# Seventy-two gathered tokens instead of eighty in a PEER expert layer, and a weight buffer moved to a later stage

## The chip, the cores and the metric

The kernel runs on one core of one Trainium2 chip. The metric is the device time of one execution in microseconds; the median of three runs of the kernel before is 1536.64 us (1535.43 to 1538.62). Five engines work at once, each through its own queue in program order: PE multiplies matrices, DVE and ACT work on elements, POOL does elementwise work and issues gathers, and SP only issues DMAs.

## The reference, cut to what matters

One layer of a decoder trunk on 512 tokens of width 1024: an input projection, 16 Mamba-2 heads and 8 latent attention heads, an output projection, a LayerNorm, and then the PEER channel mixer, which is where the change lies:

```python
def block(xb):                       # 128 tokens
    q = (xb @ w_query).reshape(T, PEER_HEADS, 2, PEER_HALF_DIM)
    s = jnp.einsum('thkd,hknd->thkn', q, sub_keys)
    sv, si = lax.top_k(s, K)
    ...
    expert_idx = jnp.take_along_axis(cand_i, top_pos, axis=-1)
    gate = jax.nn.softmax(top_s, axis=-1)
    u = jnp.take(u_table, expert_idx, axis=0)
    act = jax.nn.gelu(jnp.einsum('td,thkd->thk', xb, u), approximate=False)
    v = jnp.take(v_table, expert_idx, axis=0)
    return jnp.einsum('thk,thkd->td', gate * act, v)
```

Each token picks 8 x 16 = 128 of 16384 experts; each expert has a row of 1024 numbers in u_table and one in v_table. LayerNorm of 2^0.25 times the input plus this gives the output.

## The kernel before

The mixer is computed in two ways. The last 128 tokens are done by gathering: for each of their 128 choices a row of U per token is fetched (`row<-u,ix`, line 1587), multiplied and summed on DVE, and later a row of V likewise. The first 384 tokens (NT) are done densely, as if every token used all experts: 128 chunks of 128 experts, each chunk first "U" (the product of the chunk's 1024 x 128 weights with the tokens, GELU behind it) and later "V" (gate times GELU, times the chunk's V rows, summed over all chunks in six PSUM banks). The gates lie in a matrix of 384 tokens by 16384 experts that the kernel builds between the two from one-hot products.

Of the 384 dense tokens, the last UG = 80 have no U product. Their 128 choices each are handled by gathered U rows: UA = 64 tokens and UB = 16 tokens are spread over the partitions so that 64 + 16 = 80 gathers of 128 rows (`urow`, line 1150) and as many DVE dot products (line 1159) do all 80 x 128 of them; the results are folded into the gates. So a U product is NX = 384 - 80 = 304 columns wide. `NU` = 320 columns of each chunk's activations are kept, and the columns from NX to NU are filled with ones (line 1451).

**Products.** Every matrix product is done in fp32 quality by three passes (`mm3`, lines 90 to 92): each operand is split into a high part (ACT, line 131, `wih`) and a low part (subtraction, line 145 on DVE or POOL, line 143 on POOL, `wil`). A U chunk is 8 x 3 = 24 matmuls of 304 columns, a V chunk 18 of 512.

**The weight stream.** `Stream` loads the 512 KB weight tiles through SP's queue (`wir`, line 113). A load is issued when the subtraction of an earlier tile has freed its buffer: `self.loads(n + 1 + self.rawb)`. There are three rotating raw buffers. A fourth, `wirx` in pool `wsr`, exists from the query projection on, and then `rawb` is 4: every fourth tile uses it.

**The stages.** After the mixer's head come: the query projection with the top-16 search on DVE (about 405 to 530 us); a decode of the search's result (to about 605 us); the building of the gate matrix in 48 steps (`build_g`, to about 830 us); and the V stage to the end. U chunks fill PE beside the search, the decode and the building: 88 of them (PRE) are done before the V stage. The other 40 are done in it, one before each V chunk from V chunk GAP on, where GAP = 88 - LEAD - 1.

**Where the activations stay.** LEAD = KEEP + MORE + REST chunks of U results are held on the chip in three pools that open one after another; KEEP = 47 of them in the first. What has no place is written to DRAM (`asp<-aout`, line 1456) and read back later (line 1434): 41 chunks.

**A step of `build_g`.** DVE makes one-hot matrices (`oj`, line 1264, and `g`, line 1270) for the next step; in some steps (LOWA) ACT makes a part of `g` (line 1274). PE does 16 small f16 matmuls (lines 1308 and 1309), ACT moves their sums to `stg`, and ACT's queue stores them (`gsp<-stg`). A number of gathered dots follows on DVE: `for _ in range(3 - n % 2)`. How many U half chunks stand in a step is set by `drive`, which compares two running sums of estimated time and takes at least `least[0]` half chunks. While `beside[0]` is set (n < 32), the low part of a U tile that falls due is left to POOL: DVE writes one element of the tile (memset, line 142) so that POOL starts (line 143) while DVE is at the dots that follow. In the steps after the last dot `ug_head` puts the dots' results, which go through DRAM (`hbd`, `uw`), into the gates; its transpose is line 1197.

Before the dots, the x rows of the 16 UB tokens are spread over the partitions by DMAs into unused columns of XT: `for i in range(0, 128, UB)` (line 1542), eight DMAs on SP's queue.

Of the kernel before, what the change touches and what calls it, by code (L numbers as in the profile page):

```python
# [29 lines left out]
SCALE = 192.0 ** -0.5  # L30
NT = 384
UA = 64
UB = 16
UG = UA + UB
NX = NT - UG
NU = 320
ND = NU // 32
PIECES = 3
FIRST = 44
KEEP = 47  # L40
MORE = 12
REST = 8
LEAD = KEEP + MORE + REST
PRE = 88
# [9 lines left out]
ENDU = 9  # L54
WV = 0.86
BESIDE = 32
BSTEP = 25
GST = (1, 3, 5, 7)
LOWA = (*range(2, 32, 2), 34)
SCB = 6  # L60
# [11 lines left out]
def tile_block(ctx: ExitStack, tc: tile.TileContext, I, out):  # L72
# [6 lines left out]
    def pool(name, bufs=1, **kw):  # L79
        p = tc.alloc_tile_pool(name=name, bufs=bufs, **kw)  # L80
        opened.append(p)
        return p
# [162 lines left out]
    acd = dram.tile([64, 128], F32, name="acd")  # L245
    ixd = dram.tile([UB, 128], I32, name="ixd")
    hbd = dram.tile([128, UB], F32, name="hbd")
    asp = dram.tile([PRE - KEEP, 128, NU], F32, name="asp")

# [25 lines left out]
    beside = [False]  # L275
# [14 lines left out]
    win = Stream(wst, "wi", items, [128, 1024], raw=3, la=2, lo=lambda n: lo_on[0])  # L290
# [841 lines left out]
    def ug_index(tmp):  # L1132
# [5 lines left out]
        V.tensor_copy(UR["ix"][UA:], ix[UA:, UA:])  # L1138
        G.dma_start(ixd, ix[UA - UB:UA])
        G.dma_start(UR["g"][:UA], f(ijg[UA:, 2]))  # L1140
        G.dma_start(UR["g"][UA:], f(ijg[UA - UB:UA, 2]))
        for n in range(UROWS):
# [10 lines left out]
    def ug_dots():  # L1153
# [3 lines left out]
        for n in range(UG):  # L1157
# [4 lines left out]
            if n == 1:  # L1162
                G.dma_start(UR["ixb"], bass.AP(tensor=ixd.tensor, offset=ixd.offset, ap=[[UB, 128 // UB], [128, UB], [1, UB]]))
            if n == UA + 3:
# [76 lines left out]
    def build_g():  # L1241
# [44 lines left out]
        for n in range(48):  # L1286
            if n == BSTEP:
                next(dots)
# [40 lines left out]
            if late and late[0][0] <= n:  # L1329
                _, k, z = late.pop(0)  # L1330
# [10 lines left out]
                    lump += 1.1  # L1341
            lump += (1.45 if n + 1 in LOWA else 1.95) if n < 47 else 0.1
            if n < 32:
                keep, least[0], beside[0] = least[0], 1 + len(UO) if n % 2 == 0 else 0, n < BESIDE
                yield lump
                least[0], lump, beside[0] = keep, 0.0, False
            for _ in range(3 - n % 2):
                lump += next(dots, 0.0)
            for _ in range({34: 2, 35: 2, 36: 1}.get(n, 0)):
                lump += next(head)  # L1350
            yield lump

# [40 lines left out]
    close(mix)  # L1393
    close(zx)
    win.xp = pool("wsx")
    win.xr = pool("wsr")
    win.ha = 1
    aps = [pool("act")]
    ALL = [aps[0].tile([128, FIRST, NU], F32, name="acts")]
# [3 lines left out]

    sizes = (KEEP, MORE, REST)
    away = []
# [22 lines left out]
    def refill():  # L1428
        while away:
# [3 lines left out]
            c = away.pop(0)  # L1433
            G.dma_start(t, asp[c - KEEP])
            ACT[c] = t

    UO = {}

    def u_half(c, e, psum=None):
# [5 lines left out]
        if e:  # L1445
# [6 lines left out]
            else:  # L1452
                t = out_.tile([128, NU], F32, name="aout", bufs=3)
                A.activation(t[:, :NX], ps, AF.Gelu)  # L1454
                A.activation(t[:, NX:], one, AF.Copy)
                nc.sync.dma_start(asp[c - KEEP], t)
                away.append(c)
# [34 lines left out]
    least = [0]  # L1492
# [72 lines left out]
    B1 = gb.tile([128, 32, 8, 2], F16, name="unit")  # L1565
    least[0] = 1
    drive(build_g())
    close(gs[1], ga, gs0_, gb)
    GS = [-1, 0, 0]
# [52 lines left out]

    vst = pool("vst")
    aps.append(pool("act3"))
    fill = gather()
    next(fill)
    gt = {}
# [301 lines left out]
```

## Time and profile before

| | us |
|---|---|
| median of 3 runs | 1536.64 |
| the profiled execution, its own time | 1537.87 |
| span of its trace (first to last instruction) | 1536.1 |
| PE busy | 1503.6 |
| DVE busy | 1349.1 |
| ACT busy | 768.7 |
| POOL busy | 706.1 |

The span is what the trace shows; 1.77 us of the execution lie around it. PE's matmuls are pipelined, so one that the trace shows as 300 ns long may be followed by the next after 138 ns, and short waits can hide in PE's busy time. The granted TensorE clock has a mean of 0.996 over the span.

### The profile page before, as it was taken

To read this page: it belongs to the slowest core of one execution; us is meant where nothing else is said; L and a number is where in the kernel's file an instruction comes from. 1 tells how busy PE (TensorE), PEld (TensorE's weight loads), DVE (VectorE), ACT (ScalarE), POOL (GpSimd) and SP (SyncE) were. 2 spreads that over 40 slices of the span, in tenths; PEclk is the share of its full clock that TensorE was granted. 3 is DMA by queue.
4 is the path that set the end of the run, shared out by engine and by line. 5 is a ranking of instruction groups with operands and counts; after the bars stand their busy time and mean duration, and the time that the engine had idled before them with its cause. 6 is when DMAs were issued, how large, how long until landed. Compare 5 with 4: busy or idle time off the path is not lost.

```text
span 1536.1 us, 24889 instructions
## 1 busy us (share of the span) xinstructions
PE 1503.6 (98%) x8664; PEld 1316.1 (86%) x8664; DVE 1349.1 (88%) x2672; ACT 768.7 (50%) x1541; POOL 706.1 (46%) x522
## 2 busy tenths in 40 slices
PE   9999999999999999988999999999999999999997
PEld 7787888888888999988988988999998888888886
DVE  8979768746799999988999688999999999999998
ACT  5564477742433455665766644444444434443342
POOL 0000032420244523767852365667666676776630
PEclk9999999999999999999999999999999999999999
DMA  6243122475423676999998999999999999999994
GB/s 261 96 145 104 57 71 60 111 251 161 155 76 90 141 259 234 361 350 407 410 390 281 343 399 376 399 398 399 394 399 399 398 396 385 388 383 361 390 326 151
DMA packets 159118, 428.27 MB, mean 279 GB/s; under 512 B 18056, under 2 KB 59984, under 8 KB 158736
## 3 DMA queue, kind: packets, MB, share of 16 engines
q1 hardware_dynamic: 98336, 211.72, 39.4%
q0 software_dynamic: 55104, 196.65, 33.6%
q10 hardware_dynamic: 5552, 18.31, 3.1%
q8 instruction: 68, 1.11, 0.3%
q14 instruction: 58, 0.48, 0.1%
HBM read 393.37 MB, written 31.08 MB: 276 GB/s over the span
## 4 chain that ended last, share of the span: by engine, by line
PE 72%; DVE 11%; DMA 10%; issue 4%; ACT 3%; POOL 1%; ACTq 0%; DVEq 0%; POOLq 0%; SPq 0%
PE va L1724 9%; PE va L1720 9%; PE va L1721 9%; PE pu L91 6%; PE pu L90 6%; PE pu L92 6%; DMA row<-v,ix 3%; PE pw L90 3%; PE pw L92 3%; PE pa L91 3%; PE pw L91 3%; PE pa L92 3%; PE pa L90 3%; DVE wil L145 2%; DMA row<-u,ix 2%
## 5 line engine op out<-in xcount | busy, mean ns | idle before, releaser
L131 ACT ACTIVATE wih<-wir 128x1024 fp32r<-128x1024 f32 (+2 forms) x269 | 276.9, 1031 | 115.6 <-PE va L1724 40.7
L92 PE MATMUL pu<-XT,wil 128*128 128x304 f32 x1000 | 300.3, 300 | 4.0 <-POOL wil L143 2.6
L145 DVE TENSOR_TENSOR wil<-wir,wih 128x1024 fp32r<-128x1024 f32 (+1 forms) x212 | 256.0, 1209 | 54.2 <-ACT wih L131 34.4
L1721 PE MATMUL va<-wil,Ph 128*128 128x512 f32 x726 | 283.0, 390 | 1.6 <-DVE wil L145 1.5
L1587 POOL DMA_INDIRECT row<-v,ix x128 | 218.3, 1706 | 101.4 <-DVE ac L1608 81.4
L90 PE MATMUL pu<-XT,wih 128*128 128x304 f32 x824 | 250.0, 303 | 2.0 <-ACT aout L1454 1.6
L91 PE MATMUL pu<-XT,wih 128*128 128x304 f32 x824 | 249.6, 303 | 0.0
L1587 POOL DMA_INDIRECT row<-u,ix x128 | 175.1, 1368 | 138.3 <-DVE row L1602 71.5
L92 PEld LDWEIGHTS pu<-XT,wil 128*128 128x128 f32 x1000 | 188.3, 188 | 4.8 <-POOL wil L143 2.9
L1720 PE MATMUL va<-wih,Ph 128*128 128x512 f32 x486 | 189.1, 389 | 0.0
L1608 DVE SCALAR_TENSOR_TENSOR ac<-row,hd,ac 128x1024 f32<-128x1024 f32 x128 | 164.3, 1284 | 4.0 <-DMA row<-v,ix 2.3
L1602 DVE SCALAR_TENSOR_TENSOR row<-row,XT 128x1024 f32<-128x1024 f32 x128 | 154.1, 1223 | 11.6 <-DMA row<-u,ix 11.5
L1721 PEld LDWEIGHTS va<-wil,Ph 128*128 128x128 f32 x726 | 136.3, 188 | 30.2 <-DVE wil L145 3.3
L90 PEld LDWEIGHTS pu<-XT,wih 128*128 128x128 f32 x824 | 155.4, 189 | 4.7 <-ACT aout L1454 1.9
L91 PEld LDWEIGHTS pu<-XT,wih 128*128 128x128 f32 x824 | 155.8, 189 | 1.6
L1724 PE MATMUL va<-wih,Pl 128*128 128x512 f32 x486 | 149.9, 390 | 0.4 <-DVE Pl L1711 0.2
L145 POOL TENSOR_TENSOR wil<-wir,wih 128x1024 fp32r<-128x1024 f32 (+3 forms) x37 | 77.8, 2111 | 144.5 <-ACT wih L131 125.8
L1703 ACT ACTIVATE Ph<-P 128x384 fp32r<-128x384 f32 x121 | 63.0, 520 | 149.6 <-DVE P L1680 139.4
L1159 DVE SCALAR_TENSOR_TENSOR urow<-urow,xp 128x1024 f32<-128x1024 f32 x80 | 95.2, 1218 | 15.7 <-DMA urow<-u,uix 12.2
L1724 PEld LDWEIGHTS va<-wih,Pl 128*128 128x128 f32 x486 | 91.1, 188 | 19.9 <-DVE Pl L1711 1.2
L1720 PEld LDWEIGHTS va<-wih,Ph 128*128 128x128 f32 x486 | 91.2, 188 | 18.1
L1150 POOL DMA_INDIRECT urow<-u,uix x64 | 78.6, 1228 | 40.2 <-DVE urow L1159 23.1
(527 smaller groups left out, 3449.5 us busy)
## 6 DMA issues: line engine op xcount, KB each, us to landing
wir<-ut SPq DMA_DIRECT2D x106, 512.0 KB
wir<-v SPq DMA_DIRECT2D x86, 512.0 KB
wirx<-v SPq DMA_DIRECT2D x42, 512.0 KB
gt<-gsp SPq DMA_DIRECT2D x63, 256.0 KB
wir<-wo SPq DMA_DIRECT2D x26, 512.0 KB
wirx<-ut SPq DMA_DIRECT2D x22, 512.0 KB
gsp<-stg ACTq DMA_DIRECT2D x24, 448.0 KB
wir<-wf SPq DMA_DIRECT2D x18, 512.0 KB
```

Source lines behind the costliest of these rows:

```text
L90: T.matmul(ps, lh, rh, start=start, stop=False)
L91: T.matmul(ps, lh, rl, start=False, stop=False)
L92: T.matmul(ps, ll, rh, start=False, stop=stop)
L131: A.activation(h, r, AF.Copy)
L145: self.lo(n).tensor_tensor(l, r, h, op=OP.subtract)
L1159: V.scalar_tensor_tensor(r, r, 1.0, UR["xp"], op0=OP.mult, op1=OP.mult, accum_out=hd[:, n:n + 1] if n < UA else hb[:, n - UA:n - UA + 1])
L1587: G.indirect_dma_start(out=R[s], out_offset=None, in_=I["u"] if s < 128 else I["v"], in_offset=bass.IndirectOffsetOnAxis(ap=ix3[:, s % 128 ...
L1602: V.scalar_tensor_tensor(wide(r), wide(r), 1.0, x3, op0=OP.mult, op1=OP.mult, accum_out=hd[:, s:s + 1])
L1608: V.scalar_tensor_tensor(ac, r, hd[:, s - 128:s - 127], ac, op0=OP.mult, op1=OP.add)
L1720: T.matmul(va[b][e], Ph[b], h[:, cs], start=c == 0, stop=False)
L1721: T.matmul(va[b][e], Ph[b], l[:, cs], start=False, stop=False)
L1724: T.matmul(va[b][e], Pl[b], h[:, cs], start=False, stop=c == 127)
```

## The change

- UB is 8 instead of 16: 72 tokens of the 384 have gathered U rows, in 64 + 8 = 72 gathers and dots. The U products are 312 wide, and 8 columns are filled with ones. The x rows of the 8 tokens need 16 DMAs on SP's queue instead of 8, each half as large.
- KEEP is 50 instead of 47: 38 chunks go through DRAM instead of 41, and GAP is 17 instead of 20.
- The pool `wsr` is opened at the V stage, not after the mixer's output projection: in the query, decode and building stages there are three raw buffers, in the V stage four.
- In `build_g` a step has 2 dots, and 3 where n is a multiple of four. The number of U half chunks that stand ahead of the dots comes from the running sums alone; the POOL subtractions follow from it. BSTEP (where an extra dot is taken) is 28 instead of 25, and the last two parts of `ug_head`, its transpose and what follows it, come one step later (n = 36 and 37).

```diff
@@ -30,14 +30,14 @@
 SCALE = 192.0 ** -0.5
 NT = 384
 UA = 64
-UB = 16
+UB = 8
 UG = UA + UB
 NX = NT - UG
 NU = 320
 ND = NU // 32
 PIECES = 3
 FIRST = 44
-KEEP = 47
+KEEP = 50
 MORE = 12
 REST = 8
 LEAD = KEEP + MORE + REST
@@ -54,7 +54,7 @@
 ENDU = 9
 WV = 0.86
 BESIDE = 32
-BSTEP = 25
+BSTEP = 28
 GST = (1, 3, 5, 7)
 LOWA = (*range(2, 32, 2), 34)
 SCB = 6
@@ -1341,12 +1341,12 @@
                     lump += 1.1
             lump += (1.45 if n + 1 in LOWA else 1.95) if n < 47 else 0.1
             if n < 32:
-                keep, least[0], beside[0] = least[0], 1 + len(UO) if n % 2 == 0 else 0, n < BESIDE
+                keep, least[0], beside[0] = least[0], 0, n < BESIDE
                 yield lump
                 least[0], lump, beside[0] = keep, 0.0, False
-            for _ in range(3 - n % 2):
+            for _ in range(2 + (n % 4 == 0)):
                 lump += next(dots, 0.0)
-            for _ in range({34: 2, 35: 2, 36: 1}.get(n, 0)):
+            for _ in range({34: 2, 35: 1, 36: 1, 37: 1}.get(n, 0)):
                 lump += next(head)
             yield lump
 
@@ -1393,7 +1393,6 @@
     close(mix)
     close(zx)
     win.xp = pool("wsx")
-    win.xr = pool("wsr")
     win.ha = 1
     aps = [pool("act")]
     ALL = [aps[0].tile([128, FIRST, NU], F32, name="acts")]
@@ -1622,6 +1621,7 @@
 
     vst = pool("vst")
     aps.append(pool("act3"))
+    win.xr = pool("wsr")
     fill = gather()
     next(fill)
     gt = {}
```

On DVE, at the fourth and fifth steps of `build_g`, the order before (L1159 is a dot, L142 the memset that lets POOL start a low part, L145 a low part on DVE):

```order
L1264 TENSOR_TENSOR oj<-iotaE,jT 128x1024
L1270 TENSOR_TENSOR g<-tens,units 128x2048
L142 MEMSET wil 128x1
L1159 SCALAR_TENSOR_TENSOR urow,uhd<-urow,xp 128x1024 x3
L1264 TENSOR_TENSOR oj<-iotaE,jT 128x1024
L1270 TENSOR_TENSOR g<-tens,units 128x64x16
L142 MEMSET wil 128x1
L1159 SCALAR_TENSOR_TENSOR urow,uhd<-urow,xp 128x1024 x2
```

and now:

```order
L1264 TENSOR_TENSOR oj<-iotaE,jT 128x1024
L1270 TENSOR_TENSOR g<-tens,units 128x2048
L1159 SCALAR_TENSOR_TENSOR urow,uhd<-urow,xp 128x1024 x2
L145 TENSOR_TENSOR wil<-wir,wih 128x1024
L1264 TENSOR_TENSOR oj<-iotaE,jT 128x1024
L1270 TENSOR_TENSOR g<-tens,units 128x64x16
L142 MEMSET wil 128x1
L1159 SCALAR_TENSOR_TENSOR urow,uhd<-urow,xp 128x1024 x2
```

In the first of these steps a dot and the memset are gone, and a low part that POOL did is DVE's; the second is as it was. Over the whole program DVE has 8 dots and 8 memsets fewer and 8 low parts more; POOL has 18 low parts of line 143 instead of 26, and 8 gathers fewer.

On SP's queue, at the start of the decode, where XT gets the x rows, the order before (`wir` and `wirx` are loads of U tiles, `iaE` a small constant):

```order
L113 DMA wir<-ut 128x1024 x3
L113 DMA wirx<-ut 128x1024
L113 DMA wir<-ut 128x1024 x2
L1542 DMA XT<-xsp 16x16x64 x8
L1550 DMA iaE<-ch 128x256
L113 DMA wir<-ut 128x1024
L113 DMA wirx<-ut 128x1024
```

and now:

```order
L1486 DMA SK<-skT 128x512
L113 DMA wir<-wqr 128x1024
L113 DMA wir<-ut 128x1024 x10
L1541 DMA XT<-xsp 8x16x64 x16
L1549 DMA iaE<-ch 128x256
L113 DMA wir<-ut 128x1024 x43
L1455 DMA asp<-aout 128x320
```

The eight DMAs into XT have become sixteen, they stand one U tile earlier in the stream of loads, and the fourth buffer is gone.

On POOL, at the end of the gathers (`uixb` is the list of the UB tokens' experts), the order before:

```order
L143 TENSOR_TENSOR wil<-wir,wih 128x1024
L1150 DMA urow<-u,uix 128x1024 x2
L143 TENSOR_TENSOR wil<-wirx,wihx 128x1024
L1150 DMA urow<-u,uix 128x1024 x3
L143 TENSOR_TENSOR wil<-wir,wih 128x1024
L1150 DMA urow<-u,uixb 128x1024 x2
L143 TENSOR_TENSOR wil<-wir,wih 128x1024
L1150 DMA urow<-u,uixb 128x1024 x3
```

and now:

```order
L1150 DMA urow<-u,uix 128x1024 x2
L143 TENSOR_TENSOR wil<-wir,wih 128x1024
L1150 DMA urow<-u,uix 128x1024 x3
L143 TENSOR_TENSOR wil<-wir,wihx 128x1024
L1150 DMA urow<-u,uix 128x1024
L1150 DMA urow<-u,uixb 128x1024
L143 TENSOR_TENSOR wil<-wir,wih 128x1024
L1150 DMA urow<-u,uixb 128x1024 x7
```

The gathers of the UB tokens have become 8, and fewer low parts stand between them.

## Rows read from the trace of the kernel before

**Rows 1.** The page, part 1: busy us, share of the span, instructions.

```profile
PE 1503.6 (98%) x8664; PEld 1316.1 (86%) x8664; DVE 1349.1 (88%) x2672; ACT 768.7 (50%) x1541; POOL 706.1 (46%) x522
```

**Rows 2.** Windows: stretch, length, each engine's busy time, PEclk, DMA share, GB/s.

```profile
640.00:832.00 192.00, 177.03 (x1483) 166.82 (x1482) 175.52 (x276) 125.10 (x301) 128.67 (x95) 0.98 0.97 372
...
680.00:720.00 40.00, 38.80 (x336) 37.08 (x335) 35.38 (x56) 26.83 (x65) 33.48 (x23) 1.00 1.03 405
...
832.00:1536.00 704.00, 693.35 (x3602) 600.28 (x3601) 645.74 (x874) 308.89 (x603) 414.47 (x293) 1.00 0.98 370
```

**Rows 3.** Chain that ended last, 640 to 832 us: shares, then pieces (start, us).

```profile
by line: DMA urow<-u,uix 12.2%; issue 10.9%; DMA urow<-u,uixb 10.7%; DVE wil L145 6.6%; PE pu L90 6.4%; DVE urow L1159 6.1%; PE pu L91 5.9%; PE pu L92 5.8%; ACT g L1274 5.1%; DVE oj L1264 4.5%; ACT stg L1311 4.3%; DVE g L1270 4.0%; DMA wirx
...
743.96 2.42 POOL wil L143
...
746.40 7.22 DMA wirx<-ut
```

**Rows 4.** Lines: group, count | busy, mean ns | idle before, releasers.

```profile
L1159 DVE SCALAR_TENSOR_TENSOR urow<-urow,xp 128x1024 f32<-128x1024 f32 x80 | 95.2, 1218 | 15.7 <-DMA urow<-u,uix 12.2 <-DMA urow<-u,uixb 2.2 <-issue 1.3
...
L145 DVE TENSOR_TENSOR wil<-wir,wih 128x1024 fp32r<-128x1024 f32 (+1 forms) x212 | 256.0, 1209 | 54.2 <-ACT wih L131 34.4 <-issue 14.2 <-PE va L1721 5.2
...
L143 POOL TENSOR_TENSOR wil<-wir,wih 128x1024 fp32r<-128x1024 f32 x20 | 48.1, 2406 | 21.3 <-ACT aout L1455 5.1 <-DVE wil L142 4.8 <-ACT wih L131 4.0
...
L131 ACT ACTIVATE wih<-wir 128x1024 fp32r<-128x1024 f32 (+2 forms) x269 | 276.9, 1031 | 115.6 <-PE va L1724 40.7 <-PE pw L92 20.2 <-DMA wir<-ut 19.7
```

**Rows 5.** Timeline of PE (start, us): one V chunk, then one U chunk.

```profile
960.85 0.39 PE L1720 MATMUL va<-wihx,Ph 128*128 128x512 f32 x1
...
964.93 0.30 PE L90 MATMUL pu<-XT,wih 128*128 128x304 f32 x1
...
968.24 0.39 PE L1720 MATMUL va<-wih,Ph 128*128 128x512 f32 x1
```

**Rows 6.** Windows of the instructions on tile pu alone (PE and its count).

```profile
440.00:640.00 200.00, 122.88 (x870) 120.31 (x871) 0.00 (x0) 15.17 (x36) 1.00 0.61 193
...
640.00:832.00 192.00, 143.41 (x964) 135.67 (x963) 0.00 (x0) 16.85 (x40) 0.98 0.97 372
...
832.00:1536.00 704.00, 169.42 (x1170) 164.93 (x1169) 0.00 (x0) 20.57 (x49) 1.00 0.98 370
```

**Rows 7.** Timeline of PE in one gate step (start, us).

```profile
726.00 0.22 PE L1309 MATMUL pw<-g,oj 128*128 128x128 f16 x1
726.06 0.22 PE L1308 MATMUL pw<-g,oj 128*128 128x128 f16 x1
```

**Rows 8.** Waits of PE, 640 to 832 us: total, times, longest.

```profile
PE pw L1197 <- issue: 2.5, 1, 2.5
```

**Rows 9.** DMA of 640 to 800 us: all packets.

```profile
DMA packets 19870, 62.21 MB, mean 389 GB/s; under 512 B 2275, under 2 KB 5464, under 8 KB 19854
```

**Rows 10.** Timeline of SP's queue (start, us).

```profile
527.24 5.24 SPq L1542 DMA_DIRECT2D XT<-xsp  x8
533.87 0.34 SPq L1550 DMA_DIRECT2D iaE<-ch  x1
536.05 0.33 SPq L113 DMA_DIRECT2D wir<-ut  x1
```

**Rows 11.** Timeline of POOL and DVE at the end of a gate step.

```profile
699.42 2.40 POOL L143 TENSOR_TENSOR wil<-wir,wih 128x1024 fp32r<-128x1024 f32 x1
...
700.83 1.56 DVE L1264 TENSOR_TENSOR oj<-iotaE,jT 128x1024 f16<-128x1024 f16 x1
```

**Rows 12.** Tile oj: duration ns min/median/max, first and last start.

```profile
L1264 DVE TENSOR_TENSOR oj<-iotaE,jT x48: 677/685/2832, 591.7 to 853.8; 128x1024 f16<-128x1024 f16 x48
```

**Rows 13.** Timeline of DVE (start, us): three dots, idle time before them.

```profile
717.02 1.22 DVE L1159 SCALAR_TENSOR_TENSOR urow<-urow,xp 128x1024 f32<-128x1024 f32 x1 [0.74 <-DMA urow<-u,uix]
...
719.50 1.22 DVE L1159 SCALAR_TENSOR_TENSOR urow<-urow,xp 128x1024 f32<-128x1024 f32 x1 [1.25 <-DMA urow<-u,uix]
...
721.27 1.22 DVE L1159 SCALAR_TENSOR_TENSOR urow<-urow,xp 128x1024 f32<-128x1024 f32 x1 [0.54 <-DMA urow<-u,uix]
```

## The prediction

> **What bounds the kernel now.** I read the page first: PE is busy for 1503.6 of 1536.1 us [rows 1], so the time is PE's own work plus what PE waits for. The windows say where it waits [rows 2]: from 832 us on, in the V stage, PE has 693.35 of 704 us, and part of the rest is the tail after its last matmul; from 640 to 832 us, where the gates are built, it has 177.03 of 192. The reader is to see in the same row that DVE is at 175.52 and the DMA share at 0.97; in 680 to 720 us the DMA share is 1.03 at 405 GB/s. Three resources are nearly full there.
>
> PE's busy time hides short waits, so I count the matmuls instead. A V chunk of 18 starts at 960.85 and the next work at 964.93: 4.08 us, 226.7 ns each. A U chunk of 24 then takes 3.31 us, 137.9 ns each [rows 5]. The 964 U matmuls of 640 to 832 us [rows 6] are 132.9 us of work; the other 519 of the 1483 are nearly all small f16 ones, which follow each other after 0.06 us when nothing holds them [rows 7], about 31 us. 192 less 164 leaves 28 us in which PE waits: that is what the change can release.
>
> What holds PE there, the chain of waits tells [rows 3]: the largest parts are the gathers of U rows, 12.2% and 10.7%, and then lines of DVE. DVE works in program order without a pause except at the dots, which stood idle for 15.7 us, 14.4 of them for gathers [rows 4]. So the stretch goes at DVE's pace, DVE waits for gathers, and these come late because the DMA engines are full.
>
> **The change, part by part.**
>
> *Wider products.* From the two pitches a column costs (226.7 - 137.9) / (512 - 304) = 0.427 ns. Eight more are 3.4 ns a matmul, 82 ns a chunk, 10.5 us over 128 x 24 = 3072 matmuls. If the cost went in proportion to the columns (137.9 / 304) it would be 11.2 us, the upper end. 870 of the matmuls lie in 440 to 640 us, 964 in 640 to 832 and 1170 behind [rows 6], which leaves 68 before 440. Where PE does not wait, from 832 us on and before 440, the 1238 matmuls cost 4.2 us in full. The 1834 in between cost 6.3 us, which the 28 us of waits take in; without that cover they would count too.
>
> *Eight dots less on DVE, eight low parts more.* A dot is 1.218 us, a low part on DVE 1.209 [rows 4]; 8 against 8 cancel. Eight memsets and accumulator reads go as well: -0.5 us, between -1 and +0.3. So DVE's own work in the building stays what it was, and any gain there has to come from its waits.
>
> *Eight gathers and three stores less.* 8 x 0.524 MB and 3 x 0.164 MB are 4.7 MB. From 640 to 800 us 62.21 MB moved [rows 9]; at 405 GB/s the 4.7 MB are 11.6 us of a full DMA, the upper end. The lower end is the wait of the dots falling only with their number, 15.7 x 8 / 80 = 1.6 us. The waits come in bunches, where three dots stand in one step: three at 717.02, 719.50 and 721.27 waited 0.74, 1.25 and 0.54 us [rows 13]. Steps of three fall from 16 in 32 to 8 in 32. Half of 15.7 us is 8; with the freed DMA time I take -9.
>
> *Eight low parts less on POOL.* They take 2.406 us each [rows 4], 19 us of POOL's time, ahead of gathers in its queue. POOL itself waits, so I cost this at nothing beyond the -9.
>
> *Sixteen DMAs into XT.* Eight take 5.24 us to issue; a later DMA on the queue waits until an earlier one has landed, and the first U load behind them goes out only at 536.05, 8.8 us after the first of the eight [rows 10]. Eight more at 0.65 us could hold it for 5.2 us more; but the bytes are the same, and the queue waits for landings mostly, so it could also be nothing. What is queued behind them is the stream of U loads, now for a tile one earlier, and DVE's low part of that tile in turn holds the decode. I take +1.5, between 0 and +5.
>
> *Three raw buffers.* A load now waits for the low part three tiles back. The loop is in the chain of waits: a low part on POOL of 2.42 us, then a load of 7.22 us [rows 3], then the high part of 1.03 us [rows 4]: 10.7 us for three chunks. In 640 to 832 us a chunk takes 192 / (964 / 24) = 4.8 us, 14.3 for three. So the loop closes in time on average, and a load is late only if it takes over some 10.9 us. The chunks stand closer in the first steps, and ACT waits in order with the sums of the gate matmuls behind it. I take +2.5, between 0 and +8.
>
> *The transpose of `ug_head`.* PE waited 2.5 us for it, once, with a trip through DRAM in front of it [rows 8]. It now stands a step later: -2.5, between -2.5 and 0.
>
> *Three more held chunks.* Stores and loads beside full work; the U chunks of the V stage start three V chunks earlier, with the same work on PE. Nothing, beyond the bytes above.
>
> Sum: DVE's path through 440 to 832 us changes by -0.5 - 9 + 1.5 + 2.5 = -5.5; the transpose gives -2.5; the wider products behind and before cost +4.2. Together -3.8 us. PE's waits would be 28 - 6.3 - 5.5 - 2.5 = 13.7 us, which is possible. The profiled execution took 1537.87 us, 1.77 more than its span, so 1534.1; the median of the runs lies 1.23 below it, so 1532.8 us.
>
> **A rule that speaks against it.** At 699.42 a low part on POOL starts and runs for 2.40 us; the one-hot of DVE that starts at 700.83 takes 1.56 us [rows 11] where the median is 0.685 [rows 12], and it ends 0.57 us after POOL's. The Trainium skill, SBUF — State Buffer, "SBUF: two separate sides", says that a DVE instruction with both inputs in SBUF and a POOL instruction that reads SBUF exclude each other for the whole instruction. The trace agrees.
>
> **Rivals.**
>
> - *POOL's low parts run into the one-hots.* In the order, 13 of the 18 low parts of line 143 have only two dots as cover, before 10 of 26 had two or one. Two dots are 2.4 us, as long as the low part, so any late start falls on the one-hot, for 0.88 us at 699.42. Three more are +2.6 us: 1535.4. For it: rows 11. Against: the median of 0.685 shows that most start in time.
> - *The waits for gathers mostly stay.* The DMA engines stay full, and the dots' wait falls by a third, 5 us, instead of 9. Then -5 - 0.5 + 1.5 + 2.5 - 2.5 + 4.2 = +0.2: 1536.8. For it: 1.03 of share in 680 to 720 us; against: 8% fewer gathers a step.
> - *Late loads (the slower one).* The buffer loop gets longer than three chunks, in the first steps and after the XT DMAs: from a mean load of 10.9 us on, DVE's low parts wait for ACT's high parts. At its upper end of +8, with the gathers giving 5: -5 - 0.5 + 1.5 + 8 - 2.5 + 4.2 = +5.7: 1542.3. For it: a load of 7.22 us stands on the chain already with four buffers; against: high parts waited 19.7 us for loads in the whole program, over 269 of them [rows 4].
> - *The DMA time is the whole story.* -11.6 for the bytes, loads and XT at nothing: -11.6 - 0.5 - 2.5 + 4.2 = -10.4: 1526.2. For it: rows 2; against: DVE has to be free of waits then.
>
> **How the numbers follow.** A measurement of this kernel tells 0.2%, 3.1 us, from no change: below 1533.6 is faster, above 1539.7 slower. The forecast, with a range of its own from 1529 to 1535, has 0.38 (0.33 faster, 0.05 the same); the whole DMA time 0.12 (faster); waits that stay 0.20 (the same); the port 0.08 (0.06 the same, 0.02 slower); late loads 0.22 (0.19 slower, 0.03 the same). That makes 0.45 faster, 0.34 the same, 0.21 slower. The range from 1525 to 1542 leaves out the far ends of the late loads and of the DMA.
>
> **What would show it.** Right: a U chunk in the V stage of about 3.39 us, and a V stage longer by some 4 us; the wait before the dots down from 15.7 to about 7 us; no 2.5 us before the transpose; PE's waits in the building down to about 14 us. Late loads would show as ACT's line 131 waiting for `wir` and DVE's line 145 for ACT between 530 and 800 us; the port as one-hots of 1.5 us or more. Wrong it is if the building stage does not get shorter while the V stage gets longer.

## The result: slower by 0.9%, and the profile after

The changed kernel takes 1550.76 us (median of 6 runs, 1548.96 to 1555.26), the kernel before 1538.07 in the 6 runs beside it: ratio 1.0091, 95% interval 1.0079 to 1.0103. The forecast was 1532.8 us, with a range from 1525 to 1542. The profiled execution took 1550.99 us, with a span of 1549.2.

Part 1 of the page after, to be held against [rows 1]:

```profile
PE 1519.1 (98%) x8664; PEld 1331.7 (86%) x8664; DVE 1347.5 (87%) x2656; ACT 769.2 (50%) x1541; POOL 671.4 (43%) x503
```

The number of matmuls is the same, and PE is busy for 15.5 us longer. The windows of the kernel after, as in [rows 2]:

```profile
640.00:832.00 192.00, 184.40 (x1557) 177.58 (x1555) 177.54 (x270) 131.67 (x318) 110.89 (x85) 0.99 0.98 370
832.00:1550.00 718.00, 708.22 (x3668) 614.47 (x3668) 654.60 (x885) 313.22 (x612) 407.13 (x290) 1.00 0.98 365
```

From 640 to 832 us PE now does 1557 matmuls instead of 1483 and is busy for 184.4 us instead of 177.0: the building got denser, as forecast. The loss is elsewhere, so I lay the stages side by side, by the start of the first matmul of each:

| start of | before, us | after, us | stage longer by, us |
|---|---|---|---|
| the query projection | 397.6 | 398.6 | |
| the first U chunk behind it | 509.9 | 513.3 | 2.3 |
| the first gate matmul (step 0) | 598.2 | 613.4 | 11.8 |
| the first V matmul | 868.5 | 877.6 | -6.1 |
| the last V matmul | 1527.0 | 1540.6 | 4.5 |

The V stage came out near the forecast, and the building got 6.1 us shorter, though three raw buffers hold it up as shown below; the decode, 510 to 598 us before, lost 11.8 us. There PE stands still, once and long. The chain of waits of the kernel after through that place (start, us, what):

```profile
532.01 8.00 DMA XT<-xsp
540.03 0.65 SPq L1541
...
544.87 0.45 SPq L1549
545.43 3.76 DMA wir<-ut
549.28 1.06 ACT wih L131
550.35 1.28 ACT L1449
551.64 0.44 ACT acts L1449
552.13 0.63 PE pu L90
```

The 8.00 us are the time in which one DMA of the group, issued at 532.01, is under way until it lands. SP issues six more meanwhile; the ninth and the tenth of the sixteen each have to wait until an earlier one has landed, and the tenth goes out at 540.03. The remaining ones follow at 0.65 us each, then `iaE`, and only then the U load. ACT needs that load for its high part and has the GELU of a finished chunk queued behind it (the 1.28 us of L1449 are an ACT_TABLE_LOAD for it), so no PSUM buffer comes free, and PE waits. SP's queue after (start, us), for [rows 10], and then what SP itself waits for within the group (total us, times, longest):

```profile
531.14 13.68 SPq L1541 DMA_DIRECT2D XT<-xsp  x16
544.87 0.45 SPq L1549 DMA_DIRECT2D iaE<-ch  x1
545.43 15.18 SPq L113 DMA_DIRECT2D wir<-ut  x6
```

```profile
SPq L1541 <- DMA XT<-xsp: 2.6, 2, 1.6
```

So the group takes 13.68 us, of which 2.6 are waits for landings. In the kernel before the eight took 5.24 us, and the waits for landings came behind them. From the first DMA of the group to the next U load it is 14.3 us now (531.14 to 545.43) and was 8.8 (527.24 to 536.05): 5.5 us more. PE's own rows there:

```profile
545.00 0.30 PE L92 MATMUL pu<-XT,wil 128*128 128x312 f32 x1
552.13 0.63 PE L90 MATMUL pu<-XT,wih 128*128 128x312 f32 x1 [6.82 <-ACT acts L1449]
552.55 0.46 PE L91 MATMUL pu<-XT,wih 128*128 128x312 f32 x1
552.81 0.46 PE L92 MATMUL pu<-XT,wil 128*128 128x312 f32 x1
```

After 6.8 us without work the matmuls follow each other at 0.26 us instead of 0.143, 18 of them, some 2.1 us on top of the wait. The granted clock is the reason; the window of those six us (PEclk behind POOL's count) has it at 0.50, the lower of the two levels, 1.2 GHz:

```profile
551.00:557.00 6.00, 4.87 (x19) 4.87 (x20) 4.68 (x4) 4.13 (x9) 0.00 (x0) 0.50 0.29 94
```

The second place is the U product itself, in the V stage where PE hardly waits (to [rows 5]):

```profile
969.63 0.31 PE L90 MATMUL pu<-XT,wihx 128*128 128x312 f32 x1
...
973.08 0.40 PE L1720 MATMUL va<-wih,Ph 128*128 128x512 f32 x1
```

3.45 us a chunk, 143.75 ns a matmul; over the trace the mean is 143.5, where 137.9 became 141.3 in the forecast. And one thing that the change was not supposed to touch: the query's 384 products of 512 columns, whose moving operand is XT, take 233.3 ns each instead of 227.2, 2.3 us in all, the whole of the 2.3 us in the table. Other products of 512 columns keep their 227. In the built program XT starts 32 bytes later in every partition: it lies below the tile `one`, which has 8 columns instead of 16, and its start of 193408, a multiple of 64, became 193440.

The third is ACT. Its waits from 500 to 870 us:

```profile
ACT wih L131 <- DMA wir<-ut: 47.5, 23, 8.3
...
ACT wihx L131 <- DMA wir<-ut: 6.5, 3, 3.6
```

54 us of waiting for U loads; before it was 12.7 in the same stretch. The lines after, for [rows 4]:

```profile
L131 ACT ACTIVATE wih<-wir 128x1024 fp32r<-128x1024 f32 (+2 forms) x269 | 277.1, 1031 | 183.5 <-PE va L1724 50.4 <-DMA wir<-ut 49.4 <-DMA wir<-v 31.2
L145 DVE TENSOR_TENSOR wil<-wir,wih 128x1024 fp32r<-128x1024 f32 (+1 forms) x219 | 265.1, 1211 | 66.7 <-ACT wih L131 41.2 <-issue 21.9 <-PE va L1721 3.3
...
L1159 DVE SCALAR_TENSOR_TENSOR urow<-urow,xp 128x1024 f32<-128x1024 f32 x72 | 85.0, 1217 | 10.4 <-ACT xp L1172 3.4 <-DMA urow<-u,uix 3.3 <-ACT xp L1156 2.4
```

DVE's line 145 waits 41.2 us for ACT instead of 34.4. The dots' wait for gathers is down from 14.4 to 3.3 us, but 5.8 us are new: `xp`, the x rows that ACT copies for the dots, comes late. The 2.5 us before the transpose [rows 8] are gone. PE's waits between the first gate step and the V stage (start-to-start times beyond the usual pitch, summed) fell from about 31 to 17 us.

The rival of the one-hots has its sign in the tile's row, to be held against [rows 12]:

```profile
L1264 DVE TENSOR_TENSOR oj<-iotaE,jT x48: 669/685/1012, 605.9 to 863.3; 128x1024 f16<-128x1024 f16 x48
```

The longest one-hot takes 1.01 us where it took 2.83: none of 1.5 us or more is left.

### The profile page after: what moved, and what is told of

Its sections match the earlier page's. It is cut to its first block, busy times and chain, and to the rows that moved or that the text cites. A ratio compares the mean times of both kernels' runs of the same rounds, so it can differ in the third digit from the quotient of the medians.

```text
span 1549.2 us, 24834 instructions
## 1 busy us (share of the span) xinstructions
PE 1519.1 (98%) x8664; PEld 1331.7 (86%) x8664; DVE 1347.5 (87%) x2656; ACT 769.2 (50%) x1541; POOL 671.4 (43%) x503
## 4 chain that ended last, share of the span: by engine, by line
PE 70%; DMA 13%; DVE 8%; issue 4%; ACT 3%; POOL 2%; SPq 0%; DVEq 0%; ACTq 0%; POOLq 0%
PE va L1724 9%; PE va L1720 9%; PE va L1721 9%; PE pu L90 6%; PE pu L92 6%; PE pu L91 6%; DMA wir<-ut 4%; DMA row<-u,ix 3%; PE pw L91 3%; PE pw L90 3%; PE pw L92 3%; PE pa L91 3%; PE pa L92 3%; PE pa L90 3%; DMA row<-v,ix 3%
## 5 line engine op out<-in xcount | busy, mean ns | idle before, releaser
L145 DVE TENSOR_TENSOR wil<-wir,wih 128x1024 fp32r<-128x1024 f32 (+1 forms) x219 | 265.1, 1211 | 66.7 <-ACT wih L131 41.2
L92 PE MATMUL pu<-XT,wil 128*128 128x312 f32 x1000 | 306.8, 307 | 0.1
L1586 POOL DMA_INDIRECT row<-v,ix x128 | 212.7, 1662 | 111.8 <-DVE ac L1607 85.5
L1720 PE MATMUL va<-wih,Ph 128*128 128x512 f32 x606 | 236.4, 390 | 0.0
L90 PE MATMUL pu<-XT,wih 128*128 128x312 f32 x664 | 208.0, 313 | 11.7 <-ACT acts L1449 6.8
L91 PE MATMUL pu<-XT,wih 128*128 128x312 f32 x664 | 204.1, 307 | 0.0
L1724 PE MATMUL va<-wih,Pl 128*128 128x512 f32 x606 | 186.9, 390 | 0.6 <-DVE Pl L1711 0.5
L145 POOL TENSOR_TENSOR wil<-wir,wih 128x1024 fp32r<-128x1024 f32 (+3 forms) x37 | 78.6, 2129 | 149.2 <-ACT wih L131 122.0
L90 PEld LDWEIGHTS pu<-XT,wih 128*128 128x128 f32 x664 | 126.0, 190 | 13.9 <-ACT acts L1449 7.1
L1724 PEld LDWEIGHTS va<-wih,Pl 128*128 128x128 f32 x606 | 113.5, 188 | 25.7 <-DVE Pl L1711 1.9
L1720 PEld LDWEIGHTS va<-wih,Ph 128*128 128x128 f32 x606 | 113.7, 188 | 22.4
L91 PEld LDWEIGHTS pu<-XT,wih 128*128 128x128 f32 x664 | 126.3, 190 | 0.8
L90 PE MATMUL pu<-XT,wihx 128*128 128x312 f32 x336 | 103.5, 308 | 0.0
```

The lines of the kernel that those rows point to most:

```text
L90: T.matmul(ps, lh, rh, start=start, stop=False)
L91: T.matmul(ps, lh, rl, start=False, stop=False)
L92: T.matmul(ps, ll, rh, start=False, stop=stop)
L145: self.lo(n).tensor_tensor(l, r, h, op=OP.subtract)
L1586: G.indirect_dma_start(out=R[s], out_offset=None, in_=I["u"] if s < 128 else I["v"], in_offset=bass.IndirectOffsetOnAxis(ap=ix3[:, s % 128 ...
L1720: T.matmul(va[b][e], Ph[b], h[:, cs], start=c == 0, stop=False)
```

## The experiments

Four suspects: the columns themselves, XT's address, the sixteen DMAs, the three raw buffers. Medians of different batches were taken on different chips, so I compare by ratios to the kernel before where it matters; 0.001 is 1.5 us.

**XT's address.** In the changed kernel `one` keeps the room of 16 columns:

```diff
-    one = xt.tile([128, NU - NX], F32, name="one")
+    one = xt.tile([128, 16], F32, name="one")[:, :NU - NX]
```

> The changed kernel, but the tile of ones keeps 16 columns of room (8 are used), so that XT, which lies below it, starts at byte 193408 of a partition again (a multiple of 64), not at 193440. Theory A, the address: every matmul that streams XT pays for its start, 226.6 to 233.5 ns a matmul in the query products of 512 columns, whose width did not change. Then the query products return to 227 ns, a U matmul of 312 columns goes from 143.7 to the 141.3 ns of the forecast's slope, and the time falls by 3072 x 2.4 + 384 x 6.5 ns = 9.9 us, to 1541. Theory B, the width: 312 columns are priced like 320, because 312 is no multiple of 16 (144.7 ns by the slope). Then U stays at 143.7 ns and the time falls by 2.5 us at most.

Measured: 1546.16 us, ratio 1.0058 (1.0039 to 1.0076), 4.6 us faster. The query's products are back at 227.2 ns, but the U products only at 142.9. So the address is the query's whole loss and 0.6 ns of the U products' 5.6; neither theory had 142.9.

The other way round, the kernel before with `one` 8 columns wide and read twice:

```diff
-    one = xt.tile([128, NU - NX], F32, name="one")
+    one = xt.tile([128, 8], F32, name="one")
...
-                A.activation(t[:, NX:], one, AF.Copy)
+                A.activation(t[:, NX:].rearrange("p (a b) -> p a b", b=8), one[:, None].to_broadcast([128, 2, 8]), AF.Copy)
...
```

> The kernel before, with U products of 304, but its tile of ones has 8 columns, read twice, so that XT starts at byte 193440 as in the changed kernel. Theory A (address): the query products take 233.5 ns instead of 227, U matmuls of 304 some 2.4 ns or more above 137.9, and the time rises by 8 to 12 us less what the waits of the building take in (28 us of them): 1542 to 1548. Theory B (width): 304 is a multiple of 16 and nothing changes, 1538.

Measured: 1543.49 us, ratio 1.0030 (1.0016 to 1.0045); products of 304 columns at 139.9 ns, those of 512 at 233.35. The kernel before gets slower by 32 bytes; the copy that reads `one` twice takes 0.209 us where it took 0.208.

**The columns.** A kernel that computes no part of the mixer, run once: resident operands and nothing but chunks of 24 matmuls, one width after another, from `even` (address a multiple of 64) and `odd` (32 bytes further):

```diff
+    M0 = cs.tile([128, 16, 512], F32R, name="even")
+    cs.tile([128, 8], F32, name="edge")
+    M1 = cs.tile([128, 16, 512], F32R, name="odd")
...
+    for n in (288, 296, 304, 308, 312, 316, 320, 328, 384, 512):
+        for M in (M0, M1):
+            for _ in range(4):
+                ps = chunk(M, n)
```

> Not the mixer, and no part of the reference is computed: chunks of 24 matmuls, 128 rows, one after the other from resident operands, with 288, 296, 304, 308, 312, 316, 320, 328, 384 and 512 columns, each width from a moving operand at a multiple of 64 bytes and from one 32 bytes further, four chunks each. Theory A (address, columns at 0.427 ns): at the multiple of 64 the pitch is linear, 304 at 137.9, 312 at 141.3, 320 at 144.7, 512 at 226.7 ns; 32 bytes further every width is some ns longer, 512 by 6. Theory B (pieces of 16 columns, 64 bytes): 308, 312, 316 and 320 all have the same pitch, near 144.7, at either address, and 296 that of 304; an operand 32 bytes further touches one piece more, 16 x 0.427 = 6.8 ns, for 288, 304, 320 and 512, and nothing more for 296 and 312. The two differ at 312: 141.3 at the multiple and longer beyond by A; 144.7 at both by B.

The first matmul of some groups in its timeline (start, us); each group has 96:

```profile
64.77 0.29 PE L102 MATMUL ps<-even,wh 128*128 128x288 f32 x1
77.40 0.29 PE L102 MATMUL ps<-odd,wh 128*128 128x288 f32 x1
...
116.38 0.30 PE L102 MATMUL ps<-even,wh 128*128 128x304 f32 x1
129.62 0.30 PE L102 MATMUL ps<-odd,wh 128*128 128x304 f32 x1
143.06 0.30 PE L102 MATMUL ps<-even,wh 128*128 128x308 f32 x1
...
169.94 0.30 PE L102 MATMUL ps<-even,wh 128*128 128x312 f32 x1
183.65 0.30 PE L102 MATMUL ps<-odd,wh 128*128 128x312 f32 x1
197.42 0.30 PE L102 MATMUL ps<-even,wh 128*128 128x316 f32 x1
...
225.25 0.31 PE L102 MATMUL ps<-even,wh 128*128 128x320 f32 x1
239.33 0.31 PE L102 MATMUL ps<-odd,wh 128*128 128x320 f32 x1
253.41 0.31 PE L102 MATMUL ps<-even,wh 128*128 128x328 f32 x1
...
315.39 0.39 PE L102 MATMUL ps<-even,wh 128*128 128x512 f32 x1
337.17 0.40 PE L102 MATMUL ps<-odd,wh 128*128 128x512 f32 x1
...
359.33 0.40 PE L104 MATMUL ps<-odd,wl 128*128 128x512 f32 x1
```

A difference of two starts, divided by 96 (by 95 for the last), is the pitch. At the multiple of 64: 288 columns 131.6 ns, 304 137.9, 312 142.8, 320 146.7, 512 226.9. Between 288 and 512 that is 0.425 ns a column on average, the forecast's slope; but from 304 to 312 it is 0.61, since 304 lies 0.5 ns under the line through the ends and 312 lies 1.0 above. 32 bytes further, 304 costs 2.1 ns more, 312 0.6, 320 0.0 and 512 6.4 by its start and end. Neither theory holds: no straight line, and no equal steps of 16. What holds is the table: 4.9 ns for these 8 columns, as in the kernel.

The price of the 8 columns in the kernel, from a run with all three cures below and the same with 304 columns, which leaves out the U products of 8 tokens and keeps everything else of the change:

```diff
+NP = 304
...
-            UO[c] = [z.rearrange("p (k j) -> p k j", k=8) for z in item()] + [(psum or pu)()[:, :NX]]
+            UO[c] = [z.rearrange("p (k j) -> p k j", k=8) for z in item()] + [(psum or pu)()[:, :NP]]
...
-            mm3(ps, h[:, k], l[:, k], XTH[:, k, :NX], XTL[:, k, :NX], k == 0, k == 7)
+            mm3(ps, h[:, k], l[:, k], XTH[:, k, :NP], XTL[:, k, :NP], k == 0, k == 7)
...
```

> The run with all three edits, but the U products only 304 columns wide: the products of 8 of the dense tokens are left out, ones stand in their place. The difference to the run with all three is the price of the 8 columns alone, at the same address of XT. Theory A (a column costs 0.427 ns, the rest of the longer pitch was the address): pitch 139.5, the time falls by 10.5 us less what the waits of the building take back, so by 5 to 8 us. Theory B (width is priced in coarser pieces than a column): pitch back to 137.9 from 142.9, 15.4 us of PE's work, the time falls by 8 to 13 us.

Measured: 1525.83 us, ratio 0.9920 (0.9899 to 0.9942), against 1531.1 with 312 columns: 5.3 us. The pitch is 137.9 instead of 142.9, 15.4 us of PE's work over 3072 matmuls; PE's waits from 500 us on are about 21 us here and 11.5 there: with the wider products PE fills some 10 us that it waits here. The pitch is that of the theory of coarser pieces, the time lies in the range of the other.

**The sixteen DMAs.** One DMA in their place:

```diff
-    for i in range(0, 128, UB):
-        nc.sync.dma_start(UR["xb"][i:i + UB], wide(xsp[2, UA - UB:UA]))
+    xb_ = xsp[2, UA - UB:UA]
+    nc.sync.dma_start(UR["xb"], bass.AP(tensor=xb_.tensor, offset=xb_.offset, ap=[[0, 128 // UB], [D, UB], [64, 16], [1, 64]]))
```

> The changed kernel, but the x rows of the 8 tokens come in one DMA of the same 2048 pieces instead of 16. Theory C, SP's queue: PE's wait of 7.0 us at 545 comes from the U load that stands behind the sixteen, each of which from the ninth on waits for an earlier one to land. Then the load goes out by 537 instead of 545.4, the wait falls under 2 us, the half clock behind it goes, and the time falls by 7 to 9 us, to 1542 to 1544. Theory D, the three buffers: the load would be late anyhow, since it stands for a tile one earlier; then the wait falls to no less than 4 us and the time by no more than 3.

Measured: 1543.97 us, ratio 1.0042 (1.0028 to 1.0057), 6.8 us faster. PE's waits between 500 us and the first gate step fall from 9.7 to 4.1 us. SP's queue:

```profile
530.76 0.63 SPq L1541 DMA_DIRECT2D XT<-xsp  x1
531.45 4.30 SPq L1549 DMA_DIRECT2D iaE<-ch  x1
536.04 23.27 SPq L113 DMA_DIRECT2D wir<-ut  x7
```

The loads stream from 536.04 on. That is theory C, with 0.2 us less than its lower end of 7. The same edit in the kernel before:

> The kernel before with one edit: the x rows of its 16 tokens in one DMA instead of eight. The version with all three edits is 0.47% faster than the kernel before; this tells whether the 72 tokens or the one DMA make that. Theory C (the change's smaller number of gathers makes it): PE waits only 1.4 us between 500 us and the first step here, so one DMA gives 0 to -1 us, ratio 0.999 to 1.000. Theory D (the one DMA makes it, here as in the changed kernel, where it gave 6.8 us): ratio 0.996 to 0.997.

Measured: 1542.42 us, ratio 1.0028 (1.0013 to 1.0044): slower, which neither theory had. SP's queue:

```profile
527.17 0.73 SPq L1542 DMA_DIRECT2D XT<-xsp  x1
527.95 10.27 SPq L1550 DMA_DIRECT2D iaE<-ch  x1
```

Here the issue of `iaE` behind the one large DMA takes 10.27 us, and the decode's first `eq` waits 5.3 us for that table. So there were two explanations for what the sixteen cost: `iaE` late, or the loads late. In the changed kernel `iaE` was moved ahead of the sixteen:

```diff
-    for i in range(0, 128, UB):
-        nc.sync.dma_start(UR["xb"][i:i + UB], wide(xsp[2, UA - UB:UA]))
...
     nc.sync.dma_start(iaE.rearrange("p a b -> p (a b)"), I["ch"][:, 256:512])
+    for i in range(0, 128, UB):
+        nc.sync.dma_start(UR["xb"][i:i + UB], wide(xsp[2, UA - UB:UA]))
```

> The changed kernel with one edit: the load of iaE (the 64 KB table that the decode's eq on DVE reads first) is issued ahead of the sixteen DMAs into XT and not behind them; the weight loads still stand behind them. Theory I (the price of the sixteen DMAs is that iaE lands late and stops DVE at eq, 2.9 us, and PE behind it): eq waits for nothing, PE's wait of 7.0 us at 545 goes to 2 us or less, 4 to 6 us faster than the changed kernel, ratio to the kernel before 1.005 to 1.0065. Theory L (the price is the late weight loads behind them): 0 to 2 us faster, ratio 1.008 to 1.0095, the wait at 545 us stays at 5 us or more.

Measured: 1550.18 us, ratio 1.0077 (1.0064 to 1.0090). `eq` waits for nothing, but SP and PE show

```profile
531.40 13.04 SPq L1549 DMA_DIRECT2D XT<-xsp  x16
544.95 15.20 SPq L113 DMA_DIRECT2D wir<-ut  x6
```

```profile
PE pu L90 <- ACT acts L1449: 6.6, 1, 6.6
```

The wait of PE stays: it is the late U loads, theory L. The kernel before with one DMA and `iaE` ahead of it (the same two edits there):

> The kernel before with the x rows of its 16 tokens in one DMA and the load of iaE ahead of it. With the one DMA alone it was 4 us slower (ratio 1.0028), iaE being issued for 10.3 us behind it and DVE's eq waiting 5.3 us. Theory I (iaE's landing makes this): eq waits for nothing, no clock drop at 547 us, ratio 0.998 to 1.000. Theory L (the weight loads behind the one DMA make it): ratio 1.002 to 1.003 as before.

Measured: 1542.28 us (1537.96 to 1547.07), ratio 1.0029 (1.0017 to 1.0041). `eq` no longer waits, and PE's waits up to the first gate step fall from 7.3 to 2.9 us in the profile, yet the median does not move. That profiled execution took 1538.62 us, near the fastest of its nine, so what slows the others is not in its trace. Why one DMA costs the kernel before 4 us stays open.

**The raw buffers.** The changed kernel with `wsr` opened after the output projection again, and KEEP 47, for which there is then room:

```diff
-KEEP = 50
+KEEP = 47
...
     win.xp = pool("wsx")
+    win.xr = pool("wsr")
...
-    win.xr = pool("wsr")
```

> The changed kernel with four raw buffers from the query on and 47 held chunks, as before; 72 gathers, 312 columns and the sixteen DMAs stay. Theory C (queue): the wait at 545 shrinks by the one chunk that is loaded earlier, 3.4 us, and the late loads of the building (3.8 us at 744) go: -4 to -7, 1544 to 1547. Theory D (buffers): the wait at 545 is gone as well, -10 or more, 1541 or less. If three buffers cost nothing: 1551.

Measured: 1538.72 us, ratio 1.0009 (0.9993 to 1.0025): 12.0 us faster, the largest single cure and, by the time, theory D. ACT's waits, and then SP's queue:

```profile
ACT wih L131 <- DMA wir<-ut: 8.3, 3, 4.4
ACT wihx L131 <- DMA wirx<-ut: 0.8, 1, 0.8
```

```profile
530.49 13.31 SPq L1542 DMA_DIRECT2D XT<-xsp  x16
...
544.40 0.37 SPq L113 DMA_DIRECT2D wir<-ut  x1
```

Nine instead of 54 us; PE's waits from the first gate step to the V stage go from about 17 to 11, and the dots' wait from 10.4 to 6.8. Of the 5.8 us for `xp`, 3.1 stay (2.7 and 0.4), so loads explain only a part of that wait. In the decode the U load goes out as late as in the changed kernel, at 544.40, yet PE waits there only 1.5 us: the stall of 6.8 us takes both the sixteen DMAs and the missing buffer. The opposite, the kernel before with `wsr` opened at the V stage and nothing else:

> The kernel before with one part of the change alone: the fourth raw buffer opens at the V stage and not after the output projection, so there are three in the query, decode and building; KEEP stays 47, 80 dots, 304 columns. Theory P (the fourth buffer has a price of its own, by the stores and loads in flight): +8 to +10 us as between the runs with one DMA and aligned XT (1540.6 to 1531.1), ratio 1.005 to 1.0065, ACT's line 131 waits some 50 us on loads. Theory Q (three buffers hurt only because the changed kernel places the low parts otherwise): +2.5 us, the prediction's price, or less, ratio 1.000 to 1.002.

Measured: 1546.95 us, ratio 1.0049 (1.0030 to 1.0067), 7.5 us. Its ACT waits:

```profile
ACT wih L131 <- DMA wir<-ut: 56.6, 27, 6.7
ACT wihx L131 <- DMA wir<-ut: 20.5, 8, 3.8
```

The price does not hang on the changed order: the 1.002 at most of theory Q lie outside the interval, and theory P's range begins at 1.005.

**Together.** All three cures (old address, one DMA, four buffers with KEEP 47):

> The changed kernel with three edits at once: XT at its old address (the first of these runs alone: -4.6 us against the changed kernel), the x rows in one DMA (-6.8 us alone), four raw buffers from the query projection on with KEEP 47 (-12.0 us alone). Theory S (separate causes): the three add up, 1550.8 - 23.4 = 1527.4 us, ratio to the kernel before 0.993. Theory O (the one DMA and the four buffers cure the same late load at 530 to 560 us, where each alone took PE's waits from 9.7 to about 4 us): only one of these 6 us is gained twice over, so 1550.8 - 4.6 - 12.0 - 0.5 to 2 = 1532 to 1534 us, ratio 0.996 to 0.998, PE's waits from 500 us to the first step about 2 us. In both the pitch of the U matmuls is 142.9 ns, as with the address alone.

Measured: 1531.1 us (1530.29 to 1532.21), ratio 0.9953 (0.9937 to 0.9969): faster than both kernels. PE's waits between 500 us and the first gate step are 0.4 us. The gain is 19.7 us of the 23.4 that the three gave singly. The missing 3.7 us fit theory O, by which two of them cure the same late load, though the time is 0.9 us below its range.

The same with the three buffers and KEEP 50 left in:

> The changed kernel with XT at its old address and the x rows in one DMA; the three raw buffers and KEEP 50 stay. The difference to the run with all three edits is the price of the three buffers alone. Theory S (separate causes): 1550.8 - 4.6 - 6.8 = 1539.4 us, and the buffers alone cost 12 us. Theory O (late load at 530 to 560 us is cured by either): the buffers alone cost what they do behind 600 us, the 4 to 6 us by which PE's waits in the building fell with four buffers (16.9 to 10.8), so again about 1539 us here but only 5 to 7 us above the run with all three. The prediction had +2.5, between 0 and +8.

Measured: 1540.56 us, ratio 1.0017 (1.0004 to 1.0030), so the buffers and KEEP 50 cost 9.5 us here, more than theory O's 5 to 7 and less than theory S's 12. ACT's waits of this kernel:

```profile
ACT wih L131 <- DMA wir<-ut: 45.3, 25, 6.0
ACT wihx L131 <- DMA wir<-ut: 9.0, 6, 3.6
```

In the run with all three cures they are 2.7 us each. PE's waits from 500 us on are about 21 against 11.5 us, which is the price. On top of the cures I undid the rule for the low parts:

```diff
-                keep, least[0], beside[0] = least[0], 0, n < BESIDE
+                keep, least[0], beside[0] = least[0], 1 + len(UO) if n % 2 == 0 else 0, n < BESIDE
```

> The run with all three edits (1531.1 us) with one part of the change undone: in every second step of the building the half chunks ahead of the dots are again at least one more than those in work, so more low parts fall to POOL. Theory N (the prediction: nothing hangs on it beyond the gathers): within 2 us of 1531.1, ratio 0.994 to 0.9965. Theory P2 (POOL's low parts hold up its gathers and slow the one-hots beside them): 3 to 6 us slower, ratio 0.997 to 0.999, and the dots' wait rises from 6.8 us.

Measured: 1528.92 us (1528.55 to 1529.68), ratio 0.9931 (0.9913 to 0.9950), the fastest version with the whole work. The intervals of this run and the one without the edit overlap, so I claim only that the old rule costs nothing. It does not give POOL more to do: POOL has 18 low parts of line 143 with it and without it, 12 of `wir` and 6 of `wirx` instead of 13 and 5. So this run shows nothing of what more low parts on POOL would cost. With `iaE` ahead of the one DMA as well:

> The fastest version so far (1528.9 us: the changed kernel with XT at its old address, one DMA, four buffers, the old rule for low parts) with the load of iaE ahead of the one DMA. PE waits only 0.4 us between 500 us and the first step there and eq waits for nothing, so theory I gives 0 to -1 us, ratio 0.992 to 0.994; theory L likewise, as the loads are no later. Run as the version to beat both kernels.

Measured: 1531.35 us, ratio 0.9956 (0.9943 to 0.9969), where 0.992 to 0.994 was expected: no gain from it.

## Why the prediction was wrong

The runs split the difference of 13.0 us between after and before into the forecast's own terms:

| term | forecast, us | measured, us | from |
|---|---|---|---|
| fewer dots and gathers; transpose | -12.0 | -12.0 | 304 columns with all cures, less before |
| 8 columns | +4.2 | +5.3 | 312 less 304 columns |
| three raw buffers, KEEP 50 | +2.5 (0 to +8) | +9.5 | with less without, both with the other cures |
| sixteen DMAs | +1.5 (0 to +5) | 5.6 to 6.8 | the 10.2 us left over less the address; one DMA alone |
| address of XT | none | 3.4 to 4.6 | the same less the DMAs; address alone |
| sum | -3.8 | +13.0 | |

Each measured term is a difference of medians, good to some 2 us, and the terms add up because they are the steps from one run to the next. The split hangs on the order: with four buffers already in, one DMA and the address together give 7.6 us instead of 10.2, and the buffers 12.0 instead of 9.5. The first term comes from a kernel with one DMA, which by itself costs the kernel before about 4 us, so it may hide a larger gain; it also holds the new rule for low parts, and it keeps the three stores, which stand in the row of KEEP 50.

**The gathers and the transpose: right.** "With the freed DMA time I take -9", -0.5 for the dots and -2.5 for the transpose: -12.0. That the measured term has the same digits is luck, with the 2 us and the 4 us above. The mechanism is shown by the waits: the dots' wait for gathers fell by about 11 us, with four buffers the whole wait is 6.8 us where about 7 was forecast, and PE's waits in the building fell to about 17 us, with all cures 11, where 14 was forecast. The rival that the waits mostly stay falls. The one by which the DMA time is the whole story falls by its sum, which had loads and XT at nothing; its -14.6 for this term (-11.6 - 0.5 - 2.5) is not told apart from -12.0. The rival of the one-hots falls by its own sign: none takes 1.5 us or more.

**The wider products: the sum right, its parts not.** "From the two pitches a column costs 0.427 ns" failed: a slope over 208 columns was taken for a step of 8. The step is 4.9 ns, so PE's work grew by 15.4 us, not 10.5, above the 11.2 that I named as the upper end. The net came out at 5.3, near the 4.2, by luck: the waits took in some 10 us instead of 6.3. The Trainium skill, TensorE: Matmul & The Clock Gate, "Back-to-back issue gap", gives N / 2.4 + 2.5 ns for the isolated gap of one matmul, from which I estimate a difference of 3.3 ns for 8 columns; the runs show 4.9 in a stream of them, and they decide.

**Three raw buffers: the mechanism named, its size missed.** The step that failed is "the loop closes in time on average, and a load is late only if it takes over some 10.9 us". The runs show 26 high parts that waited for loads, 54 us in all. I put that down to chunks that come in bunches, ahead of the dots, of which an average over three chunks says nothing; no run tests this by itself. The loads were not slow: in the kernel before with three buffers they took a median of 4.4 us from issue to landing (its DMA view, 515 to 600 us), far below 10.9, and high parts waited 77 us for them. And I priced lateness by DVE's low parts and the sums of the gate matmuls behind ACT; the GELU that frees PE's PSUM buffer stands behind the high part in the same queue, and PE's largest waits, 6.8 us once and 4.7 us in two pieces, are for it. The rival of late loads had this direction, and its +8 was near the price; I gave it 0.22 because of an argument from the average.

**The sixteen DMAs: the delay right, its price missed.** "Eight more at 0.65 us could hold it for 5.2 us more" came out: the U load went out 5.5 us later after the first DMA of the group than before. The step that failed is "but the bytes are the same, and the queue waits for landings mostly, so it could also be nothing. ... I take +1.5, between 0 and +5". SP mostly issued: of 13.68 us, 2.6 were waits for landings. And the delay came through to the time in full, 5.6 to 6.8 us, because with three buffers PE had no other tile to work on: one stall of 6.8 us and 2.1 us by the lower clock behind it. With four buffers the load was as late and PE waited 1.5 us.

**XT's address: not in the sum at all.** The 8 columns less of `one` had no term, and I did not ask which tiles move in memory when it shrinks. 3072 x 0.6 ns and 384 x 6.1 ns are 4.2 us, which agrees with the runs.

What I named as proof of a wrong forecast, a building that does not get shorter while the V stage gets longer, did not come: it got 6.1 us shorter, and the V stage 4.5 longer. The forecast fell between the query and the first gate step, where I had put +1.5 us: 2.3 us of the address in the query and 11.8 us in the decode.

## What to carry to other kernels

An engine that works in order and waits for a load holds up everything behind it: price a missing buffer by what is queued behind the wait, in the steps where the work comes in bunches, not by whether the loop closes on average. When a tile changes its size, look where its neighbours in memory end up, above all the moving operands of the matmuls. Take the price of a width from a run of that width: a slope between far widths is not a step between near ones.

## What the runs showed of the hardware that was not expected

- The pitch of matmuls with fp32r operands is no straight line over the width: 288 columns 131.6 ns, 304 137.9, 312 142.8, 320 146.7, 512 226.9.
- A moving operand that starts at 32 bytes past a multiple of 64 costs some widths and others not: 512 columns 6.1 ns more in the kernel, 304 2.1, 312 0.6, 320 nothing.
- One DMA of 512 KB in pieces of 256 bytes held the issue of the next DMA on its queue for 4.30 us in the changed kernel and 10.27 in the kernel before, and what made the difference was not found.
